# Group softmax: tiles of 384 rows in a ring of four, the maxima of a tile first, split last scalings, ScalarE's loop behind five rows

## The chip, the cores and the metric

The kernel runs on one core of a Trainium2 chip. Times are device microseconds (us) of that core. A number of a whole kernel is the median of its runs. Each profile is of a single run: for the kernel before one of 1328.25 us.

## The reference

```python
def reference(x):                      # x: (4, 4096, 4352) float32
    x_g = x.reshape(B, N, 8, 544)
    x_g = x_g - x_g.max(axis=-1, keepdims=True)
    exp = np.exp(x_g)
    return (exp / exp.sum(axis=-1, keepdims=True)).reshape(B, N, D)
```

There are 16,384 rows of 17,408 B, each with eight groups of 544 elements. On the core, 128 rows (one for each partition) make one step of work, called a row below; there are 128 of these. 285 MB come in and 285 MB go out.

## The kernel before

A tile is 256 rows, two for each partition (R = 2), and there are six buffers. SyncE loads, VectorE takes the maximum of a row, ScalarE the exponentials in place with their sums, VectorE the reciprocal and the product, GpSimd stores. VectorE takes the *next* row's maximum before this row's product, so that ScalarE always has a row ahead.

```python
    # SyncE: a load when the buffer's store is done
    for t in range(nt):
        if t >= NT:
            nc.sync.wait_ge(stored[t % NT], 16 * (t // NT))
        ...
        nc.sync.dma_start(out=tile_in[:, :], in_=xt[t]).then_inc(landed[t % NT], 16)
    # the last two stores are SyncE's too
    # GpSimd: a store when both rows of a tile are scaled
    def store(t, target):
        take(nc.gpsimd, scaled, R)
        nc.gpsimd.dma_start(out=target, in_=bufs[t % NT][:, :]).then_inc(stored[t % NT], 16)
    # ScalarE: a loop of 12 rows, its start placed by head_slot
    with nc.Fori(0, turns, engines=OrderedEngineSet([nc.scalar.engine]),
                 head_slot={nc.scalar.engine: 0}):
        for s in range(S):
            scalar_exp(s)
        nc.scalar.sem_inc(max_done, -S)
    # VectorE
    vector_max(0)
    with nc.vector.Fori(0, turns):
        for s in range(S):
            ...
            vector_max(s + 1)
            vector_scale(s)
```

Of the kernel before, what the change touches and what calls it, by code (L numbers as in the profile page):

```python
# [1 line left out]

# [5 lines left out]


@with_exitstack  # L10
def kernel(
    ctx: ExitStack,
    tc: tile.TileContext,
    x: bass.AP,
    out: bass.AP,
):
    nc = tc.nc
    G = 8
    P = 128
    R = 2  # L20
    NT = 6
    S = R * NT
    xf = x.flatten_outer_dims()
    of = out.flatten_outer_dims()
    N, D = xf.shape
    Dg = D // G
    nt = N // (P * R)
    nr = nt * R
    turns = (nr - 1) // S
    LAST = 2  # L30
    ring_turns = (nt - LAST) // NT
    steps = ring_turns * NT
    f32 = mybir.dt.float32
    X = mybir.AxisListType.X
    Exp = mybir.ActivationFunctionType.Exp
    xt = xf.rearrange("(t p r) d -> t p (r d)", p=P, r=R)
    ot = of.rearrange("(t p r) d -> t p (r d)", p=P, r=R)
    turn_out = of[:steps * P * R, :].rearrange("(u b p r) d -> u b p (r d)", b=NT, p=P, r=R)

    landed = [tc.alloc_semaphore(f"landed{b}") for b in range(NT)]  # L40
    stored = [tc.alloc_semaphore(f"stored{b}") for b in range(NT)]

    max_done = tc.alloc_semaphore("max_done")
    exp_done = tc.alloc_semaphore("exp_done")
    rec_done = tc.alloc_semaphore("rec_done")
    scaled = tc.alloc_semaphore("scaled")
    last_landed = tc.alloc_semaphore("last_landed")
    last_scaled = tc.alloc_semaphore("last_scaled")
    last_stored = tc.alloc_semaphore("last_stored")

    ctx.enter_context(tc.tile_critical(no_gpsimd_drain=True))  # L51
    bufs = [ctx.enter_context(nc.sbuf_tensor(f"xt{b}", [P, R * D], f32)) for b in range(NT)]
    mx = ctx.enter_context(nc.sbuf_tensor("mx", [P, S, G], f32))
    sm = ctx.enter_context(nc.sbuf_tensor("sm", [P, S, G], f32))
    rs = ctx.enter_context(nc.sbuf_tensor("rs", [P, S, G], f32))

    def take(engine, sem, n=1):
        engine.sem_inc(sem, -n).wait_op(sem, n, "sem-ge")  # L58

    def row(s):  # L60
        b, r = divmod(s, R)
        return bufs[b][:, r * D:(r + 1) * D].rearrange("p (g d) -> p g d", g=G)

    def vector_max(n):
        s = n % S
        i = nc.vector.reduce_max(out=mx[:, s, :], in_=row(s), axis=X, negate=True)  # L66
        if n == nr - 1:
            i.wait_op(last_landed, 16, "sem-ge")
        elif s % R == 0:
            i.wait_op(landed[s // R], 16, "sem-ge")  # L70
        i.then_inc(max_done, 1)

    def vector_scale(n):
        s = n % S
        nc.vector.reciprocal(out=rs[:, s, :], in_=sm[:, s, :]).wait_op(  # L75
            exp_done, s + 1, "sem-ge").then_inc(rec_done, 1)
        xr = row(s)
        nc.vector.tensor_tensor(  # L78
            out=xr,
            in0=xr,  # L80
            in1=rs[:, s, :].unsqueeze(2).to_broadcast([P, G, Dg]),
            op=mybir.AluOpType.mult,
        ).wait_op(rec_done, s + 1, "sem-ge").then_inc(
            scaled if n < (nt - LAST) * R else last_scaled, 1)

    def scalar_exp(s):
        xr = row(s)
        for g in range(G):
            i = nc.scalar.activation(  # L89
                out=xr[:, g, :],  # L90
                in_=xr[:, g, :],
                func=Exp,
                bias=mx[:, s, g:g + 1],
                scale=1.0,
                accum_out=sm[:, s, g:g + 1],
            )
            if g == 0:
                i.wait_op(max_done, s + 1, "sem-ge")
        i.then_inc(exp_done, 1)



    for t in range(nt):
        if t >= NT:
            nc.sync.wait_ge(stored[t % NT], 16 * (t // NT))
        tile_in = bufs[t % NT]
        if t < nt - 1:
            nc.sync.dma_start(out=tile_in[:, :], in_=xt[t]).then_inc(landed[t % NT], 16)  # L108
        else:
            for r in range(R):  # L110
                nc.sync.dma_start(
                    out=tile_in[:, r * D:(r + 1) * D], in_=xt[t, :, r * D:(r + 1) * D],
                ).then_inc(landed[t % NT] if r < R - 1 else last_landed, 16)
    for k in range(LAST):
        t = nt - LAST + k
        nc.sync.wait_ge(last_scaled, (k + 1) * R)
        nc.sync.dma_start(out=ot[t], in_=bufs[t % NT][:, :]).then_inc(last_stored, 16)
    nc.sync.wait_ge(last_stored, 16 * LAST)


# [4 lines that stand above are left out]
    with nc.gpsimd.Fori(0, ring_turns) as u:  # L125
        for t in range(NT):
            store(t, turn_out[u, t])
    for t in range(steps, nt - LAST):
        store(t, ot[t])
    for t in range(nt - NT, nt - LAST):  # L130
        nc.gpsimd.wait_ge(stored[t % NT], 16 * (t // NT + 1))
    nc.gpsimd.drain()

    nc.scalar.preload_act_table(Exp)  # L134
    with nc.Fori(0, turns, engines=OrderedEngineSet([nc.scalar.engine]),
                 head_slot={nc.scalar.engine: 0}):
        for s in range(S):
            scalar_exp(s)
        nc.scalar.sem_inc(max_done, -S)
    for n in range(turns * S, nr):  # L140
        scalar_exp(n % S)


    vector_max(0)
    with nc.vector.Fori(0, turns):
        for s in range(S):
            if s == S - 1:
                for b in range(NT):
                    nc.vector.sem_inc(landed[b], -16)
            vector_max(s + 1)  # L150
            vector_scale(s)
        nc.vector.sem_inc(exp_done, -S)
        nc.vector.sem_inc(rec_done, -S)
    for n in range(turns * S, nr):
        if n + 1 < nr:
            vector_max(n + 1)
        vector_scale(n)


# [1 line left out]
_INS = ['x']  # L161
_OUTS = [((4, 4096, 4352), 'float32')]


# [23 lines left out]
```

## Time and profile before

| | before |
|---|---|
| median of the first 3 runs | 1328.16 us (1327.76 to 1328.23) |
| span of the profiled run | 1326.6 us |
| share of the two DMA queues | 51.5% + 48.2% |
| VectorE, ScalarE busy | 91%, 58% |

The main lines are in the prediction. Besides them, these are the page's lines of the DMA issues (KB each, us from issue to landing) and one line of the waits of SyncE's queue:

```profile
xt<-in_x_dram SPq DMA_DIRECT2D x63, 4352.0 KB, 41.1
out_dram<-xt POOLq DMA_DIRECT2D x62, 4352.0 KB, 51.5
```

```profile
SPq L108 <- DMA out_dram<-xt: 1213.4, 58, 62.2
```

A tile's bytes would take about 10 us alone (eight packets of 1.29 us on each engine, by the packet records); 41 and 51 us from issue to landing say that transfers stand in queues. SyncE spends nearly the whole span waiting for a store to finish, so a load starts when a buffer comes free.

Much of what follows is read from the trace's records of single DMA packets, 18,581 of them here. A record has a queue, a start, a duration and a size; its engine is not named. I put the records on 16 engines by time: a record starts 4 ns before the one ahead on its engine ends. In a check of this sorting all but about 70 records fitted within 2 ns, the first ones after a pause among them; so sums for one engine are estimates. The semaphore writes that close each transfer, one for each engine, need no such work: the sixteen of one transfer show how far the engines are apart.

### The profile page before, as it was taken

To read this page: it belongs to the slowest core of one execution; us is meant where nothing else is said; L and a number is where in the kernel's file an instruction comes from. 1 tells how busy PE (TensorE), PEld (TensorE's weight loads), DVE (VectorE), ACT (ScalarE), POOL (GpSimd) and SP (SyncE) were. 2 spreads that over 40 slices of the span, in tenths; PEclk is the share of its full clock that TensorE was granted. 3 is DMA by queue.
4 is the path that set the end of the run, shared out by engine and by line. 5 is a ranking of instruction groups with operands and counts; after the bars stand their busy time and mean duration, and the time that the engine had idled before them with its cause. 6 is when DMAs were issued, how large, how long until landed. Compare 5 with 4: busy or idle time off the path is not lost.

```text
span 1326.6 us, 2968 instructions
## 1 busy us (share of the span) xinstructions
DVE 1207.7 (91%) x384; ACT 764.5 (58%) x2049; POOL 33.3 (3%) x66
## 2 busy tenths in 40 slices
DVE  5999999999889898898998989989889898898984
ACT  3666665656555565555655556556565565555661
POOL 0000000000000000000000000000000000000000
DMA  9999999999999999999999999999999999999998
GB/s 404 420 436 430 429 435 436 436 429 431 435 435 436 430 430 435 436 436 429 431 435 435 436 430 431 434 436 436 429 431 435 435 436 431 429 435 436 431 433 351
DMA packets 18581, 570.47 MB, mean 430 GB/s; under 512 B 2064, under 2 KB 2064, under 8 KB 2064
## 3 DMA queue, kind: packets, MB, share of 16 engines
q1 hardware_dynamic: 9648, 294.13, 51.5%
q0 software_dynamic: 8928, 276.30, 48.2%
q14 instruction: 5, 0.04, 0.0%
HBM read 285.21 MB, written 285.21 MB: 430 GB/s over the span
## 4 chain that ended last, share of the span: by engine, by line
another core or an unknown queue 66%; DMA 7%; DVE 3%; SPq 1%; ACT 0%; issue 0%; POOLq 0%
DMA out_dram<-xt 4%; DMA xt<-in_x_dram 3%; DVE xt L78 1%; DVE mx L66 1%; SPq L108 1%; ACT xt L89 0%; DVE rs L75 0%; POOLq L123 0%
## 5 line engine op out<-in xcount | busy, mean ns | idle before, releaser
L89 ACT ACTIVATE xt<-xt,mx 128x544 f32<-128x544 f32 x1024 | 751.3, 735 | 539.5 <-DVE mx L66 539.5
L66 DVE TENSOR_REDUCE mx<-xt 128x8 f32<-128x4352 f32 x128 | 599.1, 4681 | 95.3 <-DMA xt<-in_x_dram 95.3
L78 DVE TENSOR_TENSOR xt<-xt,rs 128x4352 f32<-128x4352 f32 x128 | 600.6, 4692 | 4.4
L89 ACT ACTIVATION_READ_ACCUMULATOR xt<-xt,mx 128x1 f32 x1024 | 191.2, 187 | 0.0
L123 POOL DMA_DIRECT2D out_dram<-xt x62 | 33.1, 533 | 1240.3 <-POOLq L58 1240.3
L75 DVE RECIPROCAL rs<-sm 128x8 f32<-128x8 f32 x128 | 24.7, 193 | 2.6 <-ACT xt L89 2.6
L134 ACT ACT_TABLE_LOAD x1 | 1.3, 1283 | 1.0 <-SPq L51 1.0
L172 POOL MEMSET const-float32-0.0<- 128x1 f32 x1 | 0.1, 98 | 0.4 <-issue 0.4
L172 POOL MEMSET const-bfloat16-1.0<- 128x1 bf16 x1 | 0.1, 101 | 0.0
L172 POOL MEMSET const-uint8-127<- 128x1 uint8 x1 | 0.1, 99 | 0.0
L172 POOL MEMSET const-float32-1.0<- 128x1 f32 x1 | 0.1, 98 | 0.0
## 6 DMA issues: line engine op xcount, KB each, us to landing
xt<-in_x_dram SPq DMA_DIRECT2D x63, 4352.0 KB, 41.1
out_dram<-xt POOLq DMA_DIRECT2D x62, 4352.0 KB, 51.5
out_dram<-xt SPq DMA_DIRECT2D x2, 4352.0 KB, 19.3
xt<-in_x_dram SPq DMA_DIRECT2D x2, 2176.0 KB, 43.5
```

The lines of the kernel that those rows point to most:

```text
L66: i = nc.vector.reduce_max(out=mx[:, s, :], in_=row(s), axis=X, negate=True)
L75: nc.vector.reciprocal(out=rs[:, s, :], in_=sm[:, s, :]).wait_op(exp_done, s + 1, "sem-ge").then_inc(rec_done, 1)
L78: nc.vector.tensor_tensor(out=xr, in0=xr, in1=rs[:, s, :].unsqueeze(2).to_broadcast([P, G, Dg]), op=mybir.AluOpType.mult,).wait_op(rec_don ...
L89: i = nc.scalar.activation(out=xr[:, g, :], in_=xr[:, g, :], func=Exp, bias=mx[:, s, g:g + 1], scale=1.0, accum_out=sm[:, s, g:g + 1],)
L108: nc.sync.dma_start(out=tile_in[:, :], in_=xt[t]).then_inc(landed[t % NT], 16)
L123: nc.gpsimd.dma_start(out=target, in_=bufs[t % NT][:, :]).then_inc(stored[t % NT], 16)
L134: nc.scalar.preload_act_table(Exp)
L172: nc = _bacc.Bacc("TRN2", target_bir_lowering=False, num_devices=1)
```

## The change

It makes the transfers larger (packets of 52,224 B, one partition of a three-row tile, and a third fewer of them). So that VectorE does not wait, it takes the three maxima of a tile and then the three products. The first tile is loaded row by row, the last product of the last two tiles is shared by VectorE and ScalarE, and ScalarE's loop is no longer placed by head_slot: five rows stand ahead of it.

```diff
-    R = 2
-    NT = 6
+    R = 3
+    NT = 4
...
+    FIRST = 5
...
+    def scalar_scale(n, groups):     # ScalarE's half of a last product
+        for g in range(groups, G):
+            i = nc.scalar.mul(out=xr[:, g, :], in_=xr[:, g, :], mul=rs[:, s, g:g + 1])
...
+        if 0 < t < nt - 1:           # tiles 0 and the last one are loaded by rows
+            nc.sync.dma_start(out=tile_in[:, :], in_=source).then_inc(landed[t % NT], 16)
...
-    with nc.Fori(0, turns, engines=OrderedEngineSet([nc.scalar.engine]),
-                 head_slot={nc.scalar.engine: 0}):
-        for s in range(S):
-            scalar_exp(s)
+    for n in range(FIRST):
+        scalar_exp(n, n + 1)
+    nc.scalar.sem_inc(max_done, -FIRST)
+    with nc.scalar.Fori(0, turns):
+        for k in range(S):
+            scalar_exp(FIRST + k, k + 1)
...
-            vector_max(s + 1)
-            vector_scale(s)
+        for n in range(0, S, R):
+            for r in range(R):
+                vector_max(n + r)
+            for r in range(R):
+                vector_scale(n + r)
...
+        vector_scale(m, G // 2 if t >= nt - LAST else G)
```

More of the change, by code (lines that the diff above doesn't have):

```diff
@@ L6 @@
 from concourse._compat import with_exitstack
-from concourse.ordered_engine_set import OrderedEngineSet
 @with_exitstack
@@ L26 @@
     Dg = D // G
-    nt = N // (P * R)
-    nr = nt * R
-    turns = (nr - 1) // S
+    nr = N // P
+    sizes = nr // R * [R]
+    if nr % R:
+        sizes.append(nr % R)
+    nt = len(sizes)
+    turns = (nt - 1) // NT
+    FIRST = 5
     LAST = 2
@@ L35, with tile_of @@
     Exp = mybir.ActivationFunctionType.Exp
-    xt = xf.rearrange("(t p r) d -> t p (r d)", p=P, r=R)
-    ot = of.rearrange("(t p r) d -> t p (r d)", p=P, r=R)
+    def tile_of(af, t):
+        lo = t * P * R
+        return af[lo:lo + P * sizes[t], :].rearrange("(p r) d -> p (r d)", p=P)
     turn_out = of[:steps * P * R, :].rearrange("(u b p r) d -> u b p (r d)", b=NT, p=P, r=R)
@@ L46 @@
     scaled = tc.alloc_semaphore("scaled")
-    last_landed = tc.alloc_semaphore("last_landed")
+    first_landed = [tc.alloc_semaphore(f"first_landed{r}") for r in range(1, R)]
+    last_landed = [tc.alloc_semaphore(f"last_landed{r}") for r in range(1, sizes[-1])]
     last_scaled = tc.alloc_semaphore("last_scaled")
+    half_scaled = tc.alloc_semaphore("half_scaled")
     last_stored = tc.alloc_semaphore("last_stored")
@@ L66, in vector_max, with vector_scale @@
         i = nc.vector.reduce_max(out=mx[:, s, :], in_=row(s), axis=X, negate=True)
-        if n == nr - 1:
-            i.wait_op(last_landed, 16, "sem-ge")
-        elif s % R == 0:
+        r = n % R
+        if r == 0:
             i.wait_op(landed[s // R], 16, "sem-ge")
+        elif n < R:
+            i.wait_op(first_landed[r - 1], 16, "sem-ge")
+        elif n // R == nt - 1:
+            i.wait_op(last_landed[r - 1], 16, "sem-ge")
         i.then_inc(max_done, 1)
-    def vector_scale(n):
+    def vector_scale(n, groups=G):
         s = n % S
+        r = s + 1
         nc.vector.reciprocal(out=rs[:, s, :], in_=sm[:, s, :]).wait_op(
-            exp_done, s + 1, "sem-ge").then_inc(rec_done, 1)
-        xr = row(s)
+            exp_done, r, "sem-ge").then_inc(rec_done, 1)
+        xr = row(s)[:, :groups, :]
         nc.vector.tensor_tensor(
@@ L80, in vector_scale, with scalar_exp @@
             in0=xr,
-            in1=rs[:, s, :].unsqueeze(2).to_broadcast([P, G, Dg]),
+            in1=rs[:, s, :groups].unsqueeze(2).to_broadcast([P, groups, Dg]),
             op=mybir.AluOpType.mult,
-        ).wait_op(rec_done, s + 1, "sem-ge").then_inc(
-            scaled if n < (nt - LAST) * R else last_scaled, 1)
-    def scalar_exp(s):
+        ).wait_op(rec_done, r, "sem-ge").then_inc(
+            scaled if n // R < nt - LAST else last_scaled, 1)
+    def scalar_exp(n, count):
+        s = n % S
         xr = row(s)
@@ L97, in scalar_exp @@
             if g == 0:
-                i.wait_op(max_done, s + 1, "sem-ge")
+                i.wait_op(max_done, count, "sem-ge")
         i.then_inc(exp_done, 1)
+    def scalar_scale(n, groups):
+        s = n % S
+        xr = row(s)
+        for g in range(groups, G):
+            i = nc.scalar.mul(out=xr[:, g, :], in_=xr[:, g, :], mul=rs[:, s, g:g + 1])
+            if g == groups:
+                i.wait_op(rec_done, s + 1, "sem-ge")
+        i.then_inc(half_scaled, 1)
     for t in range(nt):
@@ L105 @@
             nc.sync.wait_ge(stored[t % NT], 16 * (t // NT))
-        tile_in = bufs[t % NT]
-        if t < nt - 1:
-            nc.sync.dma_start(out=tile_in[:, :], in_=xt[t]).then_inc(landed[t % NT], 16)
-        else:
-            for r in range(R):
-                nc.sync.dma_start(
-                    out=tile_in[:, r * D:(r + 1) * D], in_=xt[t, :, r * D:(r + 1) * D],
-                ).then_inc(landed[t % NT] if r < R - 1 else last_landed, 16)
-    for k in range(LAST):
-        t = nt - LAST + k
-        nc.sync.wait_ge(last_scaled, (k + 1) * R)
-        nc.sync.dma_start(out=ot[t], in_=bufs[t % NT][:, :]).then_inc(last_stored, 16)
+        tile_in, source = bufs[t % NT], tile_of(xf, t)
+        if 0 < t < nt - 1:
+            nc.sync.dma_start(out=tile_in[:, :], in_=source).then_inc(landed[t % NT], 16)
+            continue
+        others = last_landed if t else first_landed
+        for r in range(sizes[t]):
+            nc.sync.dma_start(
+                out=tile_in[:, r * D:(r + 1) * D], in_=source[:, r * D:(r + 1) * D],
+            ).then_inc(others[r - 1] if r else landed[t % NT], 16)
+    rows = 0
+    for k, t in enumerate(range(nt - LAST, nt)):
+        rows += sizes[t]
+        nc.sync.wait_ge(last_scaled, rows)
+        nc.sync.wait_ge(half_scaled, k + 1)
+        nc.sync.dma_start(
+            out=tile_of(of, t), in_=bufs[t % NT][:, :sizes[t] * D]).then_inc(last_stored, 16)
     nc.sync.wait_ge(last_stored, 16 * LAST)
@@ L128 @@
     for t in range(steps, nt - LAST):
-        store(t, ot[t])
+        store(t, tile_of(of, t))
     for t in range(nt - NT, nt - LAST):
@@ L134 @@
     nc.scalar.preload_act_table(Exp)
-    with nc.Fori(0, turns, engines=OrderedEngineSet([nc.scalar.engine]),
-                 head_slot={nc.scalar.engine: 0}):
-        for s in range(S):
-            scalar_exp(s)
+    for n in range(FIRST):
[4 more added lines that the diff above has]
+            scalar_exp(FIRST + k, k + 1)
         nc.scalar.sem_inc(max_done, -S)
-    for n in range(turns * S, nr):
-        scalar_exp(n % S)
-    vector_max(0)
+    for k, n in enumerate(range(FIRST + turns * S, nr)):
+        scalar_exp(n, k + 1)
+        if n == nr - 1 or (n + 1) % R == 0 and n // R >= nt - LAST:
+            scalar_scale(n, G // 2)
     with nc.vector.Fori(0, turns):
-        for s in range(S):
-            if s == S - 1:
-                for b in range(NT):
-                    nc.vector.sem_inc(landed[b], -16)
-            vector_max(s + 1)
-            vector_scale(s)
+        for n in range(0, S, R):
[3 more added lines that the diff above has]
+                vector_scale(n + r)
+        for b in range(NT):
+            nc.vector.sem_inc(landed[b], -16)
         nc.vector.sem_inc(exp_done, -S)
         nc.vector.sem_inc(rec_done, -S)
-    for n in range(turns * S, nr):
-        if n + 1 < nr:
-            vector_max(n + 1)
-        vector_scale(n)
+    for t in range(turns * NT, nt):
+        n, m = t * R, t * R + sizes[t] - 1
+        for k in range(n, m + 1):
+            vector_max(k)
+        for k in range(n, m):
+            vector_scale(k)
+        vector_scale(m, G // 2 if t >= nt - LAST else G)
 _INS = ['x']
```

## The prediction

> **What bounds the kernel now.** I read the page from the top: busy shares, the slices, the DMA queues, the costliest groups. Then the list of waits, the timeline of the last 40 us, and the trace's records of single DMA packets.
>
> ```profile
> span 1326.6 us, 2968 instructions
> DVE 1207.7 (91%) x384; ACT 764.5 (58%) x2049; POOL 33.3 (3%) x66
> ...
> DMA  9999999999999999999999999999999999999998
> ...
> q1 hardware_dynamic: 9648, 294.13, 51.5%
> q0 software_dynamic: 8928, 276.30, 48.2%
> ...
> L89 ACT ACTIVATE xt<-xt,mx 128x544 f32<-128x544 f32 x1024 | 751.3, 735 | 539.5 <-DVE mx L66 539.5
> L66 DVE TENSOR_REDUCE mx<-xt 128x8 f32<-128x4352 f32 x128 | 599.1, 4681 | 95.3 <-DMA xt<-in_x_dram 95.3
> L78 DVE TENSOR_TENSOR xt<-xt,rs 128x4352 f32<-128x4352 f32 x128 | 600.6, 4692 | 4.4
> ```
>
> The two DMA queues together fill 51.5 + 48.2 = 99.7% of all 16 engines' span: the kernel is bound by moving 285 MB in and 285 MB out. VectorE at 91% comes second; of its idle time 95.3 us are waits for loads, and 4.4 us stand before the scaling. ScalarE waits for maxima and has much room. So a change counts only if it changes the work of the DMA engines or makes them idle.
>
> The packet records give the finer picture. A packet of 34,816 B (one partition of a two-row tile) takes 1288 ns, one of 17,408 B (the last tile, loaded by rows) 648 ns. The difference is 640 ns for 17,408 B, 27.2 GB/s for one engine, and the fixed part of a record is 8 ns; consecutive records overlap by 4 ns, so a packet costs 4 to 5 ns beyond its bytes. Each transfer closes with a semaphore write per engine, some 6 to 13 ns more. On 15 engines a tile's load and store take 20.57 us, which is 16 x 1280 = 20,480 ns of bytes plus 90 ns of such costs. One engine is slower, about 20.65 us per tile from a third of the way on: in the last store 15 engines finish by 1321.5 us and the sixteenth at 1324.7. It has queued work without a gap from 2.07 us to there, so **this engine sets the end**.
>
> ```profile
> 1291.71 18.63 SPq L117 DMA_DIRECT2D out_dram<-xt  x2
> ...
> 1294.32 4.69 DVE L66 TENSOR_REDUCE mx<-xt 128x8 f32<-128x4352 f32 x1 [2.64 <-DMA xt<-in_x_dram]
> ...
> 1299.15 4.69 DVE L78 TENSOR_TENSOR xt<-xt,rs 128x4352 f32<-128x4352 f32 x1
> ...
> 1305.04 0.20 DVE L75 RECIPROCAL rs<-sm 128x8 f32<-128x8 f32 x1 [1.20 <-ACT xt L89]
> 1305.27 4.69 DVE L78 TENSOR_TENSOR xt<-xt,rs 128x4352 f32<-128x4352 f32 x1
> ```
>
> That is the last row: maximum, exponentials, scaling until 1309.96, then its store. Stores issued earlier keep the engines at work meanwhile; the 15 fast ones pause about 0.6 us near 1310.5, the slow one not at all. There is almost nothing at the end to win.
>
> [...] with half-size load packets at the end, loads and stores still alternate one for one, and two-row stores then land every 15.5 us (8 x (0.64 + 1.28) = 15.4) instead of 20.6. [...] the slow engine is there in this trace, its cause isn't shown. [...] The trace has only five packets of instructions in the whole span, so today no loop refetches.
>
> **The change, part by part.**
>
> (1) Tiles of three rows. The bytes stay: 128 rows x 2 directions x 139,264 B for each engine / 27.2 GB/s = 1310.7 us. Packets on each engine: before, 63 x 8 + 16 in + 64 x 8 out = 1032. After, 24 (first tile by rows) + 41 x 8 + 16 in, and 42 x 8 + 8 out = 712. 320 fewer x 4.5 ns = **-1.4 us**. Transfers fall from 65 + 64 = 129 to 46 + 43 = 89, 40 x 8 ns = **-0.3 us**. The slow engine: its excess over the others, by the spread of the last landings, is 3.2 us, and about 5 us by its own packet records. If it goes with packets, it falls by a third, 1 to 1.8 us; if with bytes, not at all. I take **-0.9 us**.
>
> (2) Maxima of a tile first. VectorE's work stays at 9.43 us a row in the timeline (4.60 + 0.22 + 4.61 from start to start), 28.3 us a tile, against 3 x 10.32 = 31.0 us of DMA. Does it wait for ScalarE now? One row of exponentials takes 764.5 / 128 = 5.97 us. From the tile's start: maxima end at 4.7, 9.3 and 13.9; exponentials end at 10.7, 16.6 and 22.6; scalings would start at 13.9, 18.7 and 23.6. Each row is ready 3.2, 2.1 and 1.0 us early. No wait, 0 us.
>
> (3) Four buffers for six; the bytes held are the same. With 31.0 us a tile, a buffer's circle is 4 x 31 = 124 us: load 31 at half rate, work 29, store 31; 33 us are left for standing in queues. Followed through the start (first row in at about 8.7 us, first store moving at about 43.5, all four loads done at 85), this settles with a load issued about 11 us before the one ahead ends and a store issued about 22 us before. Neither queue runs dry: 0 us.
>
> (4) First tile by rows. The first maximum starts at about 14.28 - 5.15 = 9.1 us. But the DMA engines load without a pause there anyway, and the first store, now of three rows, moves at 43.5 us, as the old one did at 45. 0 us.
>
> (5) ScalarE's loop. A row is 16 instructions (1024 + 1024 over 128 rows), twelve rows 192, five rows ahead 80; [...] 0 us.
>
> (6) The end. Let L be the landing of the last three-row tile on the slow engine. The two last rows' load packets (0.64 us) alternate with store packets of 1.92 us: row 126 takes 8 x 2.57 = 20.5 us, and row 127, once the older stores have run out at about L+34, is in at about L+35.6. The store of the three-row tile stands behind it in the same queue and takes 15.4 us, to L+51. Beside it VectorE: maximum of row 127 from L+36.1 to 40.7, exponentials to 46.7, the half scaling (4.69 / 2 = 2.35) and ScalarE's other half (four of some 0.73 us) to L+50, store moving 1.1 us after its issue (1309.99 to 1311.1 before): L+51.3. An idle gap of about 0.3 us; if the multiplication needs another activation table (a load was 1.28 us), some 1.6. I take **+0.6 us**.
>
> Sum: -1.4 - 0.3 - 0.9 + 0.6 = -2.0, so 1328.16 - 2.0 = **1326.2 us**.
>
> **The rivals.** First, a new wait at the end: my gap of 0.3 us is a difference of two sums of some 50 us. If VectorE comes 3 us later or the older stores end earlier, the engines stand still for that long: 1329. For it: the last tile is computed with all maxima first, and the last store can only start then. Against it: the last scaling is halved. Second, ScalarE's loop refetches at each of 10 turns. [...] But VectorE has 2.7 us of slack in every tile, 11 in a turn, and stores 22 us of queue. Hidden; the time would stay at 1326 to 1327. Third, the coarser ring starves: were one queue empty at times, the other would take the full rate, as the trace's last stores show, so only both empty cost anything; a DMA idle of 1% would make it 1340. The queue sums speak against it. Fourth, the intent, a real gain: it is capped. At 27.2 GB/s without any other cost the bytes alone are 1310.7 us, plus 2.07 us before the first packet and 1.9 after the last one: 1315 us of span, about 1316 timed, 0.9% off. So over 2% faster is out of reach.
>
> **Range and chances.** The small terms add to -3.6 at best (slow engine relieved by its 1.8 us, no gap) and +3 with a late tail[...]. 8 in 10: 1323.5 to 1330. Over 2% faster would be below 1301.6, under the floor: 1%. Over 2% slower, above 1354.7, needs a starved ring or packets of 52 KB being split or slowed: 2%. Within 2%: 97%.
>
> **What would show it.** Packets of 52,224 B at 1928 ns and about 12,820 records in all (712 + 89 on each of 16 engines); queue shares again summing to 99.5% or more; VectorE's scaling without idle time before it in the middle, its maxima waiting about 2.6 us a tile for loads; tiles landing every 30.8 to 30.95 us; five or six instruction packets, not tens; the last store's start within 2 us of the end of the one before. Packets longer than 1928 ns, VectorE waiting for ScalarE in each tile, or a DMA digit below 9 in the middle slices would prove me wrong.

Passages that no trace or run here shows are cut from it, and the cuts are marked. The sum came to -1.4 - 0.3 - 0.9 + 0.6 = -2.0 us, so 1326.2 us.

## The result, and the profile after

The changed kernel took 1328.7 us (1328.11 to 1329.23, 4 runs) against 1328.2: the same, ratio 1.0004 with a 95% interval of 0.9987 to 1.0022. The time lies in the predicted range, but the 2.0 us of gain at its centre did not come.

From the page of the changed kernel: span, engines, packets, queues (packets, MB, share), groups and issues.

```profile
span 1327.3 us, 2856 instructions
...
DVE 1202.0 (91%) x384; ACT 760.6 (57%) x2057; POOL 22.1 (2%) x45
...
DMA packets 12820, 570.46 MB, mean 430 GB/s; under 512 B 1424, under 2 KB 1424, under 8 KB 1424
...
q1 hardware_dynamic: 6912, 296.36, 51.8%
q0 software_dynamic: 5904, 274.07, 47.7%
q14 instruction: 4, 0.03, 0.0%
...
L75 DVE TENSOR_REDUCE mx<-xt 128x8 f32<-128x4352 f32 x128 | 592.1, 4679 | 106.0 <-DMA xt<-in_x_dram 106.0
L91 DVE TENSOR_TENSOR xt<-xt,rs 128x4352 f32<-128x4352 f32 x128 | 596.0, 4656 | 4.4
...
xt<-in_x_dram SPq DMA_DIRECT2D x41, 6528.0 KB, 44.8
out_dram<-xt POOLq DMA_DIRECT2D x41, 6528.0 KB, 49.2
```

The packets are as counted (12,820). The queues fill 99.5%, VectorE still waits only for loads, and there are four instruction packets. The parts that were meant to cost nothing cost nothing, yet a third fewer packets bring no time. This is one tile on VectorE in the middle of the span (start, duration, engine, line, operation; in brackets the idle time before it):

```profile
923.54 13.87 DVE L75 TENSOR_REDUCE mx<-xt 128x8 f32<-128x4352 f32 x3 [2.51 <-DMA xt<-in_x_dram]
937.33 0.20 DVE L88 RECIPROCAL rs<-sm 128x8 f32<-128x8 f32 x1
937.56 4.69 DVE L91 TENSOR_TENSOR xt<-xt,rs 128x4352 f32<-128x4352 f32 x1
942.17 0.19 DVE L88 RECIPROCAL rs<-sm 128x8 f32<-128x8 f32 x1
942.40 4.69 DVE L91 TENSOR_TENSOR xt<-xt,rs 128x4352 f32<-128x4352 f32 x1
```

Three maxima, then products back to back; the only idle time is the 2.5 us before the tile has landed. The end of the changed kernel:

```profile
1291.27 22.93 SPq L144 DMA_DIRECT2D out_dram<-xt  x2
...
1300.16 4.68 DVE L75 TENSOR_REDUCE mx<-xt 128x8 f32<-128x4352 f32 x1 [4.63 <-DMA xt<-in_x_dram]
...
1310.87 0.20 DVE L88 RECIPROCAL rs<-sm 128x8 f32<-128x8 f32 x1 [1.19 <-ACT xt L103]
1311.11 2.42 DVE L91 TENSOR_TENSOR xt<-xt,rs 128x2176 f32<-128x2176 f32 x1
1311.11 2.67 ACT L120 ACTIVATE xt<-xt,rs 128x544 f32<-128x544 f32 x4 [0.27 <-DVE rs L88]
```

The last product is done at 1313.78. The packet records say what the DMA engines do then: 15 of them finish the store before the last by 1311.8 us and stand idle some 4 us; the sixteenth finishes it at 1315.2, starts the last store in the same instant and ends at 1325.5. In the kernel before the slowest engine ended at 1324.7. In both kernels **one DMA engine is never idle and sets the end**, so the question is what that engine did with the time it should have saved.

The records answer it. A record of 52,224 B should take 1928 ns (3 x 640 + 8, from the records before), and 95% do. But now and then records on many engines at once, mostly of loads, take 60 to 730 ns longer. I call this a burst. Summed over all 16 engines and all records after 100 us (the start is alike in both), the time above nominal is 6.5 us before and 37.9 us after. On the engine that ends last, stretches of over 30 ns come to 4.1 us, some 1.9 us of it after 1270 us, where the loads end. The stretched time is no overlap: between 597 and 603 us there are 16.04 records in flight on average, as ever, and 418 GB/s, against 433 for 500 to 560 us. In the windows of the changed kernel this dip looks like this (us, busy time of VectorE, ScalarE and GpSimd, clock, DMA share, GB/s; with the bytes of each packet spread over its time, both neighbours are at 434):

```profile
560.00:597.00 37.00, 34.39 (x11) 23.77 (x65) 0.53 (x1) 1.00 0.99 430
597.00:603.00 6.00, 5.93 (x5) 6.00 (x17) 0.00 (x0) 1.00 1.00 418
603.00:640.00 37.00, 34.33 (x12) 20.80 (x58) 0.53 (x1) 1.00 1.01 438
```

The DMA share stays at 1.00 in the dip; only the rate shows it.

### The profile page after: what moved, and what is told of

Its sections match the earlier page's. It is cut to its first block, busy times and chain, and to the rows that moved or that the text cites. A ratio compares the mean times of both kernels' runs of the same rounds, so it can differ in the third digit from the quotient of the medians. Undisturbed runs are those within 1.5% of the kernel's fastest.

```text
span 1327.3 us, 2856 instructions
## 1 busy us (share of the span) xinstructions
DVE 1202.0 (91%) x384; ACT 760.6 (57%) x2057; POOL 22.1 (2%) x45
## 2 busy tenths in 40 slices
DMA packets 12820, 570.46 MB, mean 430 GB/s; under 512 B 1424, under 2 KB 1424, under 8 KB 1424
## 3 DMA queue, kind: packets, MB, share of 16 engines
q0 software_dynamic: 5904, 274.07, 47.7%
## 5 line engine op out<-in xcount | busy, mean ns | idle before, releaser
L75 DVE TENSOR_REDUCE mx<-xt 128x8 f32<-128x4352 f32 x128 | 592.1, 4679 | 106.0 <-DMA xt<-in_x_dram 106.0
L151 POOL DMA_DIRECT2D out_dram<-xt x41 | 21.9, 535 | 1240.1 <-POOLq L67 1240.1
L120 ACT ACTIVATE xt<-xt,rs 128x544 f32<-128x544 f32 x8 | 5.3, 737 | 1.6 <-DVE rs L88 1.6
```

Of the source, the lines that this page charges most:

```text
L75: i = nc.vector.reduce_max(out=mx[:, s, :], in_=row(s), axis=X, negate=True)
L120: i = nc.scalar.mul(out=xr[:, g, :], in_=xr[:, g, :], mul=rs[:, s, g:g + 1])
```

## The experiments

Each is told by its edit against the changed kernel, unless it says otherwise. Stretch is the sum over 16 engines, after 100 us, of what packet records lie above nominal, in the one profiled run. The rounds ran on different chips (again to one_row_tiles on one, two_row_tiles to stores_from_scalar_three_rows on a second, the last four on a third), so times of different rounds are best compared through the kernel before.

| run | median us (range, runs) | before, same rounds | ratio | stretch us |
|---|---|---|---|---|
| before | 1328.2 (1327.76 to 1328.25, 4) | | | 6.5 |
| changed | 1328.7 (1328.11 to 1329.23, 4) | 1328.2 | 1.0004 | 37.9 |
| again | 1328.89 (1325.47 to 1336.09, 5) | 1328.01 | 1.0000 | 60.4 |
| interleaved | 1334.33 (1328.99 to 1347.07, 6) | 1328.01 | 1.0066 | 7.9 |
| two_row_interleaved | 1328.94 (1328.49 to 1329.03, 5) | 1328.01 | 1.0006 | 6.3 |
| one_row_tiles | 1335.21 (1334.59 to 1335.50, 5) | 1328.01 | 1.0052 | 8.4 |
| two_row_tiles | 1389.66 (1389.56 to 1389.76, 4) | 1327.96 | 1.0466 | 571 |
| whole_first_tile | 1334.39 (1329.69 to 1336.51, 6) | 1327.96 | 1.0044 | 48.4 |
| stores_from_scalar_two_rows | 1327.54 (1326.70 to 1328.36, 5) | 1327.96 | 0.9998 | 5.4 |
| stores_from_scalar_three_rows | 1327.94 (1327.76 to 1328.75, 5) | 1327.96 | 1.0004 | 21.3 |
| one_row_packets | 1329.84 (1329.50 to 1331.38, 5) | 1327.78 | 1.0017 | 4.2 |
| loop_over_three_blocks | 1339.78 (1334.18 to 1341.62, 6) | 1327.78 | 1.0086 | 47.7 |
| two_row_whole_first | 1328.23 (1327.86 to 1328.74, 5) | 1327.78 | 1.0004 | 4.4 |
| two_row_whole_last | 1331.11 (1330.85 to 1331.26, 5) | 1327.78 | 1.0024 | 5.9 |

### again: do the bursts come back?

No edit.

> The changed kernel once more, unchanged. In its first trace some load packets of 52,224 B were stretched in bursts: summed over 16 engines the packet records lay 68 us above nominal, before 35 us (2.1 us per engine more), and that is about what my predicted gain of 2.0 us lost. Theory A (the bursts belong to the kernel: same addresses and same phases each time): the bursts come back at the same times (168, 597, 1113, 1238 and 1281 us), total excess 60 to 75 us, time 1328.7 within 0.7. Theory B (chance, something outside the kernel): bursts at other times or none, excess anywhere from 35 us up; in a run without them the time is near 1326.5.

The bursts came back at other times (350, 474, 567, 783, 901 us and more) and in another amount: 92 us above nominal over the whole span, outside the 60 to 75 of theory A. One run took 1325.47 us and another 1336.09, while eleven runs of the kernel before lay within 0.8 us. So *when* a burst comes is chance. That they come with this kernel and not with the one before is not: its runs scatter over 10.6 us. The fastest run lies near the predicted centre.

The trace is of the slowest run, and with the first trace it shows what the stretch does within one and the same kernel. At the load landing at 1260 us the last engine was 10.7 us behind the first, against 5.0 in the first trace. So the last row landed 7.2 us later (1307.3 against 1300.1), as the maximum that waited for it shows (beside 1300.16 in the first trace):

```profile
1307.31 4.69 DVE L75 TENSOR_REDUCE mx<-xt 128x8 f32<-128x4352 f32 x1 [4.79 <-DMA xt<-in_x_dram]
```

Fifteen engines then stood idle for some 7 us before the last store, the sixteenth finished the store ahead at 1322.35, and the run took 7.2 us more (1336.09 against 1328.92).

### interleaved: is the new order to blame?

```diff
+    vector_max(0)
     with nc.vector.Fori(0, turns):
-        for n in range(0, S, R):
-            for r in range(R):
-                vector_max(n + r)
-            for r in range(R):
-                vector_scale(n + r)
+        for s in range(S):
+            ...
+            vector_max(s + 1)
+            vector_scale(s)
```

> The changed kernel with the old order on VectorE (the next row's maximum, then this row's scaling), all else as changed. My step (2) says the order costs nothing: the same time as the changed kernel within 1 us (1328 to 1329.5), VectorE not waiting for ScalarE in either. A rival in which the order matters (buffers come free later as the three scalings come last) would have it some us faster.

This expectation missed: 1334.33 in the median and a range of 18 us. VectorE waited for ScalarE 2.3 us in all (1.2 in the changed kernel), so the order itself costs nothing on VectorE, as I had reckoned. In its one trace, of a run of 1329.20 us, there was little stretch after 100 us, but three engines had each lost about 5 us in bursts between 50 and 105 us (4.5, 4.6 and 5.2): the second store landed within 0.7 us on 13 engines and 9.4 to 9.7 us later on three, while their loads were only about 2 us late. An engine that has fallen behind stays behind: nearly 900 us later the three were still 9.6 to 10 us late with their stores. The slow runs, up to 1347.07, were not traced. The scatter is there with either order; whether the old order makes bursts likelier is open, six runs of such scatter don't tell.

### two_row_interleaved and one_row_tiles: the size alone

```diff
# on top of interleaved
-    R = 3            -    NT = 4
+    R = 2            +    NT = 6       # two_row_interleaved
+    R = 1            +    NT = 12      # one_row_tiles
```

> The changed kernel with tiles of two rows, six buffers and the old order: what is left of the change are the first tile by rows, the split last scalings and ScalarE's loop. By packet counts against three rows: 320 packets more per engine x 4.5 ns + 40 transfers x 8 ns = +1.8 us, slow engine up to +1.8 us; so 2 to 3.5 us slower than a three-row kernel without bursts. If the bursts come with packets of 52 KB (theory A), it shows an excess near 35 us and a time equal to the kernel before within 1 us or lower (1327 to 1328.5).

> Tiles of one row, twelve buffers, old order, packets of 17,408 B. Each engine has 2048 packets and 256 transfers, against 1032 and 129 with two rows: 1016 x 4.5 ns + 127 x 8 ns = +5.6 us. If the slow engine's excess (3 to 5 us) goes with packets it doubles: +3 to +5 us more, so 1337 to 1339; if with bytes or time, 1333 to 1334. VectorE's order and work are unchanged, so nothing else should move; the stretch excess should be no more than with two rows.

The time from one load's landing to the next on the engine that lands first is, in the median, 10.327 us for a one-row tile (one_row_tiles), 20.567 for two rows (the kernel before) and 30.807 for three (interleaved; the other traces with long packets have 30.807 to 30.817). Less the bytes (10.240 us a row) that leaves 87 ns a tile each time: 16 packets and 2 semaphore writes. So the packets cost what I said, and three rows against two save 87 x (64 - 42.7) = 1.9 us on each engine. One row takes 6.3 us more than two (1335.21 against 1328.94), where packets and semaphores give 87 x 64 = 5.6. The excess of the slowest engine did not double, then, and 1335.2 lies between the two numbers that I had put down; it goes neither with packets nor with bytes as I had imagined it. Both kernels have little stretch and runs within 0.9 us. Two rows took 0.9 us more than the kernel before: within the 1 us that I had put down, but above the 1328.5.

### one_row_packets: the coarse tile or the long packet?

```diff
-        return af[lo:lo + P * sizes[t], :].rearrange("(p r) d -> p (r d)", p=P)
+        return af[lo:lo + P * sizes[t], :].rearrange("(r p) d -> p r d", p=P)
```

and the buffers viewed alike, for loads and stores. Tiles, order, ring and ends stay as changed; only the packets are cut in three, and their rows lie 128 rows apart.

> The changed kernel, tiles of three rows as changed, but a partition takes three rows that lie 128 rows apart, so that each packet is 17,408 B instead of 52,224 B; order, buffers, transfers and ends stay. Packets per engine 2048 instead of 712: 1336 x 4.5 ns = +6.0 us. If scatter and bursts belong to the long packets: runs within 1 us of each other and 1332 to 1335, little stretch after 100 us. If they belong to the coarse tile and its order: runs scattered over 4 us or more, median 1334 to 1340.

The bursts are gone: 4.2 us of stretch, of which 0.6 us in pieces of over 30 ns, and runs within 1.9 us, as wide as those of the kernel before on this chip (1327.17 to 1329.08). It is not the chip: loop_over_three_blocks, in the same rounds on it, has the long packets and 47.7 us of stretch. The time of 1332 to 1335 that I had put down was too high. So the coarse tile, the ring of four and the order of VectorE do not make them; the long packets, or the addresses they walk, do. The engine that lands first takes 30.958 us a tile, 151 ns more than with long packets: that is 32 packets more, so 4.7 ns for each, and then 87 - 16 x 4.7 leaves 6 ns for a semaphore write. Over 42.7 tiles the cut costs 6.4 us, and yet the kernel took only 1.1 us more than the changed one's 1328.7 (0.9 more than the 1328.89 of its second set of runs; 1.6 and 1.2 with the kernels before of the same rounds). About 5 us, then, are what the bursts take in a median run, by this reckoning. As an estimate from these numbers, a three-row kernel without them would take 1329.84 - 6.4 = 1323.4 us.

### two_row_tiles: why the order needs three rows

```diff
-    R = 3            -    NT = 4
+    R = 2            +    NT = 6
```

with the maxima of a tile first.

> The changed kernel with two-row tiles and six buffers, but maxima of a tile first as changed. By my working of step (2), with two rows ScalarE comes late: maxima end at 4.7 and 9.2 us, exponentials at 10.7 and 16.7, so VectorE waits about 1.4 us per tile before the first scaling and some more before the second, and a tile takes 21.4 to 21.6 us on VectorE against 20.6 on the DMA engines. VectorE becomes the bound: 64 x 21.5 + about 20 of start and end = 1385 to 1400 us, 4.5% to 5.5% slower. A rival in which the order costs nothing at any tile size: 1329, as with the old order.

1389.66 us, within the range. First the waits of this kernel (who waited for what: us in all, times, longest), then one tile on VectorE, then three windows:

```profile
DVE rs L88 <- ACT xt L103: 150.3, 128, 1.4
DVE mx L75 <- DMA xt<-in_x_dram: 9.2, 2, 8.7
```

```profile
907.72 9.27 DVE L75 TENSOR_REDUCE mx<-xt 128x8 f32<-128x4352 f32 x2
918.42 0.20 DVE L88 RECIPROCAL rs<-sm 128x8 f32<-128x8 f32 x1 [1.43 <-ACT xt L103]
918.65 4.69 DVE L91 TENSOR_TENSOR xt<-xt,rs 128x4352 f32<-128x4352 f32 x1
924.28 0.20 DVE L88 RECIPROCAL rs<-sm 128x8 f32<-128x8 f32 x1 [0.93 <-ACT xt L103]
```

```profile
300.00:600.00 300.00, 266.04 (x85) 165.71 (x449) 7.44 (x14) 1.00 1.00 422
600.00:900.00 300.00, 266.02 (x85) 165.71 (x451) 7.44 (x14) 1.00 1.00 417
900.00:1200.00 300.00, 266.03 (x85) 165.72 (x449) 7.44 (x14) 1.00 1.00 416
```

ScalarE comes 1.43 and 0.93 us late in every tile, the tile takes 21.40 us on VectorE (907.72 to 929.12), and VectorE is the bound: it hardly waits for loads. And the DMA share still reads 1.00. The engines move just 416 to 422 GB/s, their records being stretched by 571 us in all. These are packets of 34,816 B, so stretch as such does not need the long ones. Here it may be spare time: 21.40 - 20.57 = 0.83 us a tile on each of 16 engines is some 850 us in all. No run tells whether it is the same thing as a burst. A DMA share of 1.00 is therefore no proof that the DMA engines are the bound; the rate and who waits for whom are.

### stores_from_scalar_two_rows and stores_from_scalar_three_rows: is it the software queue?

The first is an edit of the kernel before, the second of the changed one. GpSimd's stores go; ScalarE issues the store of a tile next to its first row of the following tile (there FIRST is 2 and 3).

```diff
     def store(t, target):
-        take(nc.gpsimd, scaled, R)
-        nc.gpsimd.dma_start(out=target, in_=bufs[t % NT][:, :]).then_inc(stored[t % NT], 16)
+        take(nc.scalar, scaled, R)
+        nc.scalar.dma_start(out=target, in_=bufs[t % NT][:, :]).then_inc(stored[t % NT], 16)
```

> The kernel before with one change: stores are issued by ScalarE [...] rather than GpSimd (software queue). In the kernel before, one engine ends 3.2 us after the others, and its longer packets are mostly stores of the software queue; besides, loads are stretched by 15 us over 16 engines while the first store is being made ready. If the software queue is the cause of both: 3 to 4.5 us faster, 1323.5 to 1325, last landings of all engines within 1 us of each other. If one engine is slow for another reason: 1327 to 1328 and the spread stays.

> The changed kernel with its stores issued by ScalarE. If the bursts of stretched loads come with the software queue, they vanish: total excess of packet records under 20 us over 16 engines, runs within 1 us of each other, and 1322 to 1325. If they belong to packets of 52 KB, the runs still scatter over 5 us or more and the excess stays at 30 to 70 us; median 1325 to 1331.

With two rows the stretch of the stores is halved (2.3 us in place of 4.7 after 100 us), and the slowest engine ends 0.8 us after the others in place of 3.2. But the time is that of the kernel before (0.9998): the median is 0.4 us lower, not the 3 to 4.5 expected. The stretch of loads as the first store starts is still there (19.4 us over 16 engines between 20 and 60 us, 15.5 before), so GpSimd's queue (q0, software_dynamic on the page of the kernel before) is not its cause. The theory holds for part of the spread of the engines, and fails for the time.

With three rows the expectation holds in one half. The runs lie within 1.0 us, and no 100 us between 100 and 1200 have more than 1.8 us of stretch, where the two traces of the changed kernel have up to 4.0 and 6.7. Yet interleaved, with GpSimd's stores, has no more than 0.8 there in its one trace, so one quiet trace proves little. And there is still a burst at the end of the loads: 13.3 of the 21.3 us come between 1270 and 1300 us, as do 13.9 of 37.9 in the changed kernel's first trace and 8.6 of 60.4 in its second. So the runs speak for bursts in the middle that go with long packets *and* GpSimd's queue, without showing it; the one at the end does not need that queue. It sets the last engine back further (its load landing is 3.7 us after the first one's at 1260 us and 5.9 us at 1290), which is of the size of the 1.9 us of fewer packets: 1327.94 us, no gain.

### whole_first_tile, two_row_whole_first: does the start reach the end?

```diff
-        if 0 < t < nt - 1:
+        if t < nt - 1:
```

in the changed kernel, and in two_row_interleaved.

> The changed kernel with its first tile loaded as one transfer. I predicted 0 us for loading it by rows. New theory: by rows, the first store starts some 8 us earlier, takes DMA time from the loads, and so the last rows land later while fewer stores are left to cover the last tile's computing: the 15 fast engines idle about 4 us before the last store. Then loading it whole makes the last rows land about 4 us earlier and that idle time nearly vanishes, and the time is 0 to 3 us lower (1325.5 to 1328.5), as far as bursts allow. If the start doesn't reach the end, the same time and the same 4 us idle.

> Two-row tiles in the old order with the first tile loaded whole, last scalings split: against two_row_interleaved (1328.9 us, little scatter) only the first tile's load differs. Theory: by rows, the first store moves about 8 us earlier and the last rows land about 6 us later (1299.6 us against 1293.8 in the kernel before), and all engines stand idle about 5 us before the last store. Whole: last rows land near 1294 us, the slow engine has no idle time, 0.5 to 1.5 us faster: 1327.4 to 1328.4. If the start doesn't reach the end: 1328.9 again.

With three rows the expectation missed: 1334.39 us and a range of 7 us. The records show bursts again, one of them at 51 us, and engines that drift apart: the first store's landings are spread over 3.4 us, those of the store at 1207 us over 23, those of the load at 1202 us over 6. Scatter of that size buries an effect of 3 us, so this run says nothing about the first tile. With two rows, where nothing scatters, the theory holds: the last row lands at 1294.2 us in place of 1299.6, the slowest engine has no idle time, and the time is 1328.23 against 1328.94. Part of that is the other chip, though: set against the kernel before of the same rounds, 0.9 us too much become 0.5. In two_row_interleaved the earlier first store takes DMA time from loads; the last load then lands 5.4 us later (1299.6 against 1294.2), with fewer stores left to cover the last tile's computing.

### two_row_whole_last: what the split product is worth

```diff
# on top of two_row_interleaved
-        vector_scale(n, G // 2 if half else G)
+        vector_scale(n)
```

and ScalarE's half removed.

> Two-row tiles in the old order, first tile by rows, but the last scalings whole on VectorE: against two_row_interleaved (1328.9 us) only the split is undone. There the DMA engines wait for the last scaling, so it counts in full: 4.69 us on VectorE instead of 2.67 on ScalarE beside 2.42 on VectorE: +2.0 us, 1330.9. If the split didn't matter: 1328.9.

1331.11 against 1328.94: +2.2 us, or 2.4 with the kernels before of the same rounds, for the 2.0 expected. Here, where all engines wait for the last product, splitting it counted in full. In the changed kernel's trace the slowest engine does not wait for it, so there it counts for nothing.

### loop_over_three_blocks: is a refetch hidden?

```diff
-    FIRST = 5
+    FIRST = 8
...
-    with nc.scalar.Fori(0, turns):
-        for k in range(S):
+    with nc.scalar.Fori(0, 4):
+        for k in range(2 * S):
```

> The changed kernel with ScalarE's loop of 24 rows behind 8 rows ahead [...]: 4 turns. If a turn refetches: some 12 to 24 more instruction packets of 8 KB[...]. My rival says that this is hidden by VectorE's 2.7 us of slack a tile and the stores' queue: the same time as the changed kernel within its scatter (1325 to 1336). If ScalarE's loop mattered, 10 us or more above that.

That ScalarE's loop lies in three blocks, as the label has it, is shown by no trace; the 12 to 24 packets were my estimate.

1339.78 us, 11 us above the changed kernel, and outside its scatter but for one run. From the page, the queue of instruction fetches, and from the waits:

```profile
q14 instruction: 23, 0.19, 0.0%
```

```profile
DVE mx L75 <- DMA xt<-in_x_dram: 113.2, 40, 9.0
ACT xt L103 <- issue: 5.9, 3, 2.0
DVE rs L88 <- ACT xt L103: 4.0, 4, 1.2
```

23 fetches of 8 KB in place of 4. What my rival said of the engines is true: ScalarE stalled for 5.9 us in all, VectorE waited 4.0 us for it, and beside its 113.2 us of waits for loads that alone would be hidden, by my estimate. But a fetch is itself a packet on the bound resource. Each leaves a gap of some 0.3 us in the data of one DMA engine (8,192 B took 309 ns on the engines amid the data, before and after), and lengthens its next packet by 0.12 us on average (0 to 0.25): 19 x 0.42 = 8 us. The landings show one engine falling behind the rest: its load landing is 0.3 us after the fifteenth at 180 us, 4.3 us at 551, 10.5 at 859 and 12 us at 1230; stretches add to the 8 us. The page shows this as 0.0% of the engines' time. It is 0.0% of sixteen, and near a per cent of the one that sets the end. So the length of ScalarE's loop and what stands ahead of it, which I had put at 0 us, can count. The changed kernel's loop, of twelve rows behind five, fetches no more than the one before: 4 packets against 5.

## Why the prediction was right or wrong

The range (1323.5 to 1330) held the time, and 97% for "within 2%" was right; the reason was right too, that the bytes leave only 0.9% to be won. The gain at the centre, -2.0 us, did not come: +0.5. That the time lay within the range was partly luck: of the nine runs of this kernel two lie above it (1330.16 and 1336.09). By its steps, on the engine that ends last:

- **Step (1), fewer packets, -1.4 - 0.3 us:** shown, as 1.9 us on every engine (10.269 against 10.284 us a row). The -0.9 us for the slow engine was no worse a guess: it takes 20.65 us a tile to the others' 20.57 before, and 30.89 to 30.81 after, for most of the span; that is 0.08 us a tile in both, hence about 0.08 x (64 - 42.7) = 1.7 us less, were it so for the whole span. Why that engine is slow is not settled; with one-row tiles its excess did not grow with the packets.
- **What failed is a term that the sum did not have.** The step "The bytes stay: ... / 27.2 GB/s" took it that a packet of 52,224 B moves at the rate of one of 34,816. It mostly does, but the bursts cost the slowest engine 4.1 us, where the kernel before has next to none. -1.9 - 1.7 + 4.1 = +0.5, an estimate as far as the 1.7 goes, and the slowest engine ended 0.7 us later than before. Of the prediction's own signs of being wrong, "packets longer than 1928 ns" is the one that came. My section on the range named "packets of 52 KB being split or slowed", as the way to over 2%; at 0.3% it is what happened.
- **Step (2), the order:** right. VectorE waits 1.2 us for ScalarE in the whole span; with two-row tiles the same working gave 1.4 us of wait per tile, and the trace has 1.43.
- **Step (3), four buffers:** right, the queues fill 99.5% and one engine never idles.
- **Step (4), the first tile by rows, 0 us:** too simple. It moves idle time to the end, about 0.5 us with two rows; on the slowest engine of the changed kernel's trace nothing.
- **Step (5), the loop, 0 us:** right for this loop, at 4 instruction packets; it was an estimate. **The second rival**, that a refetch would be hidden, was wrong: +11 us for 19 fetches more, by my reckoning through the DMA engine (8 us) and not through ScalarE.
- **Step (6), the end:** the schedule was right to a us. From the landing L of the last three-row tile (1264.4 us), row 126 landed at L+20.9 (20.5 predicted), row 127 at L+35.4 (35.6), the store ahead was through at L+50.8 (51.0) and the last product at L+49.4 (50). No second activation table was loaded (one ACT_TABLE_LOAD in the span, of 1.28 us, at its start). The gap on the slowest engine was 0, not the +0.6 that I took. **The first rival**, a late end, is there on the other 15 engines, which idle about 4 us, and costs nothing in this trace because they aren't the last; with more stretch, in the trace of again, the end came 7.2 us later.

What stays open is what a burst is. Among the kernels whose pace the DMA engines set, only those with packets of 52,224 B have it (one_row_packets has none); it hits loads more than stores (19 us to 5 in the first trace of the changed kernel between 100 and 1285 us, 48 to 5 in the second); it seems rare in the middle once ScalarE issues the stores (no 100 us between 100 and 1200 over 1.8 us of stretch, one trace; five runs within 1.0 us); and when it strikes differs from run to run. Whether the stretch of two_row_tiles, with shorter packets, is the same thing is open too. Whether length or address decides was not told apart. None of the kernels run here beats the kernel before by more than the noise; the nearest, with ScalarE's stores and two rows, has a ratio of 0.9998.

## What to carry to other kernels

In a kernel bound by DMA, reckon the end from the slowest of the sixteen engines: an engine that fell behind here, by slow packets (interleaved: three engines 9.4 to 9.7 us late at the second store, 9.6 to 10 us nearly 900 us later) or by instruction fetches (loop_over_three_blocks: 0.3 us late at 180 us, 12 us at 1230), stayed behind, and the mean share of the page did not show it (0.0% for the fetches). Larger packets saved only their fixed cost here (4.7 ns each), so compare the saving with the scatter that they may bring (runs over 10.6 us in again), and time such a change over many runs. A DMA share of 1.00 is no proof of a DMA bound (two_row_tiles: 1.00 at 416 to 422 GB/s, with VectorE the bound); look at the rate and at who waits for whom.
